# Projection operands 14 columns later, low weight parts 64 bytes later, one tile of ones in place of two

## The chip, the cores and the metric

The kernel runs on one core of one Trainium2 chip. The metric is the device time of one execution in microseconds (us); lower is better. Names used below: TensorE is PE (matmuls) with its weight loads as PEld; VectorE is DVE, ScalarE is ACT, GpSimd is POOL, SyncE is SP. L295 is line 295 of the kernel. SBUF is the memory on the chip, 128 partitions side by side; PSUM is where matmuls write their sums.

## What is computed

One layer of a hybrid decoder over 16 learned tokens and 1024 tokens of 1024 channels (T = 1040), in float32. Cut to what matters:

```python
h = layer_norm(concat([meta, x]), g, b)
z = h @ w_in + b_in                      # split into q | k | v | conv input | two gates
a = swa_sink_attention(q, k, v, ...)     # 8 heads of 64, window 128
y_attn = a @ w_attn_proj                 # 512 -> 1024
c = c_val * sigmoid(c_gate)
c = silu(layer_norm(causal_dwconv(c), g, b))
y_conv = c @ w_conv_proj                 # 512 -> 1024
mixed = sigmoid(g_attn) * y_attn + sigmoid(g_conv) * y_conv
h = layer_norm(ALPHA * h + mixed @ w_out, g, b)
up = causal_dwconv(h @ ffn_w_up); u, g = split(up)
out = layer_norm(ALPHA * h + (gelu(g) * u) @ ffn_w_down, g, b)
```

## The kernel before, in words

**Three products for one.** To keep float32 accuracy at the faster rate of the float32r format, an operand is split into a high part (the value rounded to float32r) and a low part (what is left). One product of two operands is then three matmuls: high weights by high operand (L295), high weights by low operand (L299), low weights by high operand (L300). The function `product` issues these three for each chunk k of 128 channels, and all of them add up in one PSUM tile. In a matmul one operand of 128 x 128 is loaded into PE first (the weights, a LDWEIGHTS in the profile), and the other one, 128 x up to 512 columns, streams past it (the moving operand). The load for the next matmul runs while the present one streams.

**The z stage** (from about 57 us to 416 us, L303 to L882). There are 30 tiles of 128 output channels of z. For each, `weights` (L274) takes a raw tile of 128 x 1024 from the pool `wraw`, loads it by SP, takes two tiles `whi` and `wlo` from the pool `wsp`, and splits: ACT copies the high part, DVE or, from the 24th tile, POOL subtracts for the low part. Only the third tile, which is used while a later one is already loading, has tiles of its own. `z_group` (L303) then makes 24 matmuls (8 chunks of three) for each of three groups of columns: ZG (0 to 400, 400 to 784, 784 to 1040), or TG, whose first group begins at column 14. The normalised input lies in the tiles RHO (chunks 0 to 3) and RHC (4 to 7) in slots of T = 1040 columns, high and low parts in turn. The attention over eight blocks of queries and the depthwise convolution (31 multiply-adds of 1026 columns per chunk on DVE, L663) run between these tiles. The sum over the conv chunks (L882) is split (L893, L894) and multiplied by a tile of ones on PE (L885, L886) for the mean; squares follow the same way (L946 to L949), then scaling, the activation, and the split into OC (L972, L973). Attention results are scaled and split into OA (L984 to L986).

**The projections** (416 to 514 us, L1071 to L1118). OA holds the attention result, OC the conv result: four chunks each, in eight slots of T columns, high and low in turn, of which columns 0 to 1026 of a slot are used. Eight tiles of weights (`weights` again, with both projections in one tile) are multiplied with four groups of columns, PG: 0 to 258, 258 to 514, 514 to 770, 770 to 1026. For each group 12 matmuls read OA and 12 read OC. `merge` multiplies with the gates on DVE.

**What follows.** Output rows (`out_rows`, 514 to 611 us), the up projection (L1481, to about 1052 us; seven products per block of channels in place of eight, each of 12 matmuls of 258 columns and 12 of 256), the down projection (L1614, 512 columns). They reuse OA, OC, RHO and RHC with offsets of their own, and the `wsp` tiles: `prep_wo` for two chunks of `w_out` (L1051), a ring of split weights in the up projection (L1299), rows of gains and sums in the down projection (L1637).

**What sets the order.** A scheduler places the instructions of each engine in a fixed order, by the ranks that the code sets (`rank`, `tc.cur_priority`); extra edges (`after`, `pin`, `line`) fix the order in places. Each engine then works through its own list and waits for the others by semaphores.

**Memory.** Pools on the left side, in this order: const, small, wraw, wsp, arena (FA, RHC, RHO, OB), and OA behind them. Each tile in `wsp` is 128 x 1024 (4096 bytes in a partition), two buffers for each of the two tags. Two tiles of ones, 128 x 128, lie in const: `ones` in float32, filled by DVE (L222) and used by 28 matmuls at the start (L535), and `ones_r` in float32r, copied from it by ACT (L892) and used for the means.

Of the kernel before, what the change touches and what calls it, by code (L numbers as in the profile page):

```python
# [23 lines left out]
F = mybir.dt.float32  # L24
R = mybir.dt.float32r
# [4 lines left out]
P = 128  # L30
D = 1024
KC = D // P
NMETA = 16
S = 1024
T = S + NMETA
U0 = 14
# [65 lines left out]
def tile_hybrid_layer(  # L102
# [3 lines left out]
    nc = tc.nc  # L106
# [5 lines left out]
    def load(o, i):  # L112
        return nc.sync.dma_start(out=o, in_=i)
# [5 lines left out]
    def f32(ap):  # L119
        return ap.bitcast(F)  # L120

    def after(ins, first):

        tc.add_manual_dep(ins.ins, first.ins.name, mybir.DependencyInfo(
            mybir.DependencyClass.NoSync, mybir.DependencyReason.SCHED_ONLY), reason="order of work")

    @contextmanager
    def rank(p):

        saved = tc.cur_priority  # L130
        tc.cur_priority = p
        yield
        tc.cur_priority = saved


    const = ctx.enter_context(tc.tile_pool(name="const", bufs=1, side="left"))
    small = ctx.enter_context(tc.tile_pool(name="small", bufs=4, side="left"))
    wraw_p = ctx.enter_context(tc.tile_pool(name="wraw", bufs=2, side="left"))
    wsp_p = ctx.enter_context(tc.tile_pool(name="wsp", bufs=2, side="left"))
# [28 lines left out]
    sp = start.enter_context(tc.tile_pool(name="start", bufs=1, side="right", reuse_waits="tile"))  # L168
# [49 lines left out]
    ffw = lambda t, c: cff[:, t * 44 + c:t * 44 + c + 1]  # L218

    ones_r = const.tile([P, P], R, name="ones_r")  # L220
    ones = const.tile([P, P], F, name="ones")
    nc.vector.memset(ones, 1.0 / CW)  # L222
    qb = const.tile([P, 4], F, name="qb")
    half_ = const.tile([P, 1], F, name="half")
# [34 lines left out]

    tc.cur_priority = RK_QKV  # L260

    def wraw(shape):
        return wraw_p.tile(shape, F, name="wr", tag="wr")

    def split(raw, hi, lo, quick=False, behind=None):
        ins = nc.scalar.copy(hi, raw)  # L266
        if behind is not None:
            after(ins, behind)
        return (nc.vector if quick else nc.gpsimd).tensor_tensor(lo, raw, f32(hi), OP.subtract)  # L269
# [4 lines left out]
    def weights(shape, fill):  # L274
        fills[0] += 1
        n = fills[0]
        own = n == 3
        raw = sp.tile(shape, F, name="wr3") if own else wraw(shape)
        with rank({1: 13, 2: 18, 3: 17, 4: 23}.get(n, RK_SPLIT)):
            last_fill.append(fill(raw))  # L280
        hi, lo = (sp.tile(shape, R, name=t + "3") if own else wsp_p.tile(shape, R, name=t, tag=t)
                  for t in ("whi", "wlo"))
        if n <= 3:
            return hi, lo, raw
        with rank(RK_SPLIT):
            last_split.append(split(raw, hi, lo, n <= 23))
        return hi, lo
# [22 lines left out]
    def z_tile(fill, groups, evac, wt=None):  # L310
        wt = wt or weights([P, KC, P], fill)
        for g, (a, b) in enumerate(groups):
            z_group(wt, g, a, b, evac)
# [156 lines left out]
    def parts(g, *ks, hi_act=()):  # L470
        a, b = HG[g]
        for k in ks:
# [5 lines left out]
            dv(V.tensor_tensor(h0(k, 1, a, b), tm, f32(h0(k, 0, a, b)), OP.subtract))  # L478

    first = [weights([P, KC, P], in_cols(m)) for m in (4, 5, 0)]  # L480
    evacs0 = [k_evac, v_evac, q_evac(0)]

# [125 lines left out]

    tc.cur_priority = RK_QKV + 3000
    wt_c1 = [weights([P, KC, P], in_cols(m)) for m in (11, 7)]  # L610
    tc.cur_priority = RK_RESID
    residual(3, -1, 0, 1, 2, 3)
# [93 lines left out]
    for q4 in range(2):  # L706
        ps = pat.tile([P, 512], F, name="ps_v4", tag="t", bufs=2)
        for i in range(4):
            c = NMETA + (q4 * 4 + i) * P
            nc.tensor.transpose(ps[:, i * P:(i + 1) * P], vT[:, c:c + P], ident)  # L710
        src = ps[:, :].rearrange("p (n g d) -> p n g d", g=2, d=HD)
        for g in range(NKV):
            hi, lo = (V[:, q4 * 4:q4 * 4 + 4, g, i] for i in range(2))
# [30 lines left out]
    for h in range(NH):  # L744
        g, r = divmod(h, 4)
        o = ps[:2, h * 16:(h + 1) * 16]
# [137 lines left out]
    def mean_mms(ps, w, hi, lo):  # L884
        nc.tensor.matmul(ps, w, hi, start=True, stop=False)  # L885
        nc.tensor.matmul(ps, w, lo, start=False, stop=True)  # L886
# [2 lines left out]
    c_hi = cp.tile([P, 16 + T], R, name="c_hi", tag="cin")  # L889
    c_lo = Kx[0].rearrange("p n c -> p (n c)")[:, :U]  # L890
    with rank(RK_EVAC):
        nc.scalar.copy(ones_r, ones)  # L892
        nc.scalar.copy(c_hi[:, :U], csum)  # L893
        pinned.append(nc.vector.tensor_tensor(c_lo, csum, f32(c_hi[:, :U]), OP.subtract))  # L894
        for g, (a, b) in enumerate(UG):
            means[g] = pat.tile([P, 512], F, name="ps_m", tag="st"[g % 2], bufs=2)
            mean_mms(means[g][:, :b - a], ones_r, c_hi[:, a:b], c_lo[:, a:b])
# [6 lines left out]
    OC = late.tile([P, 8320], R, name="OC")  # L904
# [8 lines left out]
    def temp(n):  # L913
        return tmp_p.tile([P, 386], F, name="t", tag="t", bufs=6)[:, :n]


    def conv(c, hl, a, b):
        o = (c * 2 + hl) * T
        return OC[:, o + a:o + b]

    def pin(ins):

        if pinned:
            after(ins, pinned[-1])
        pinned.append(ins)
# [9 lines left out]
    def cln_var(g):  # L935
        a, b = UG[g]
        n = b - a
        s_ = temp(n)
        nc.scalar.activation(s_, acc[0][:, a:b], AF.Square)
        for c in range(1, CH):  # L940
            q_ = temp(n)
            nc.scalar.activation(q_, acc[c][:, a:b], AF.Square)
            pin(dve.tensor_tensor(s_, s_, q_, OP.add))

        hi, lo = (OC[:, i * T + a:i * T + b] for i in (2, 3))
        pin(dve.tensor_copy(hi, s_))  # L946
        pin(dve.tensor_tensor(lo, s_, f32(hi), OP.subtract))
        sums[g] = pat.tile([P, 512], F, name="ps_m", tag="s", bufs=2)
        mean_mms(sums[g][:, :n], ones_r, hi, lo)  # L949
# [24 lines left out]


    def oo(r, hl, a, b):
        o = (r * 2 + hl) * T
        return OA[:, o + a:o + b]

    def o_split(g, r):  # L980
        a, b = UG[g]
        n, x = b - a, 2 if g == 0 else 0
        t = o_all[:, r, a:b]
        pin(dve.tensor_tensor(t[:, x:], t[:, x:], inverse[r][:, a + x - 2:b - 2], OP.mult))  # L984
        pin(dve.tensor_copy(oo(r, 0, a, b), t))
        pin(dve.tensor_tensor(oo(r, 1, a, b), t, f32(oo(r, 0, a, b)), OP.subtract))  # L986
# [7 lines left out]
    cln_centre(0)  # L994
    cln_centre(1)
    cln_var(0)
    cln_centre(2)
    cln_var(1)
    cln_rstd(0)
    cln_scale(0)  # L1000
    cln_var(2)
    cln_rstd(1)
    cln_scale(1)
# [41 lines left out]
    def prep_wo(k, raw=None, behind=None):  # L1045
        if k < 4:
            hi, lo = OA[:, k * 2048:k * 2048 + 1024], OA[:, k * 2048 + 1024:k * 2048 + 2048]
        elif k < 6:
            hi, lo = ((RX, RW)[k - 4][:, x:x + 1024] for x in (0, 1024))
        else:  # L1050
            hi, lo = (wsp_p.tile([P, D], R, name=n, tag=n) for n in ("whi", "wlo"))  # L1051
        if raw is None:
            raw = wraw([P, D])
            load(raw, w_out_v[k])
        split(raw, hi, lo, k < 4, behind)
        wo[k] = (hi, lo)
# [16 lines left out]
    for m in range(KC):  # L1073
        hi, lo = weights([P, KC, P], lambda raw: load(raw, w_ab[m]))
# [37 lines left out]
        if m in (2, 3):  # L1112
            raw = (FA[:, 4112:5136], OB[:, 3072:4096])[m - 2]
            load(raw, w_out_v[m + 2])
            prep_wo(m + 2, raw, last_act)
# [38 lines left out]
    def line(ins):  # L1154

        if lined:
            after(ins, lined[-1])
        lined.append(ins)
        return ins
# [129 lines left out]
    RING = [RHO[:, i * 1024:(i + 1) * 1024] for i in range(4)]  # L1289
# [4 lines left out]
    def wsplit(src):  # L1294
        i = ring_next[0]
        ring_next[0] += 1
        i %= len(RING)
        if RING[i] is None:
            RING[i] = wsp_p.tile([P, D], R, name="ws", tag=("whi", "wlo")[i % 2])  # L1299
        t = RING[i]  # L1300
        hi, lo = t[:, 0:512], t[:, 512:1024]
        nc.scalar.copy(hi, src)  # L1302
        ins = nc.vector.tensor_tensor(lo, src, f32(hi), OP.subtract)  # L1303
        if pinned_w[0]:
            line(ins)
        elif ring_next[0] <= 10:
            after(ins, formed[0])
        return hi, lo
# [7 lines left out]
    def up_weights():  # L1316


        def tt(*x):
            ins = nc.vector.tensor_tensor(*x)  # L1320
            if pinned_w[0]:
                line(ins)

        rows = w_rows(0)
        for c in range(FC):
            a11, a12, a21, a22 = rows
            yield wsplit(a11)
            yield wsplit(a12)
            p4 = wsplit(a22)
            tt(a22, a21, a22, OP.add)  # L1330
            tt(a21, a11, a21, OP.subtract)
            tt(a11, a22, a11, OP.subtract)
            yield wsplit(a11)
            yield p4
            yield wsplit(a22)
            tt(a22, a12, a11, OP.subtract)
            yield wsplit(a21)
            p3 = wsplit(a22)
            if c + 1 < FC:
                rows = w_rows(c + 1)  # L1340
            yield p3
# [117 lines left out]
    for c in range(FC):  # L1459
        V4, X, Z, Y = (pup.tile([P, 1024], F, name=n, tag=n) for n in ("pw", "px", "pz", "py"))  # L1460
        passes = ((1,), (0,)) if c == 0 else ((0, 1),)
        for subs in passes:
            last = subs == passes[-1]
            w_next = iter(range(7))
            a, b = SUB[subs[0]][0], SUB[subs[-1]][1]
# [168 lines left out]
    extra = []  # L1634

    def ln_rows(names):
        return [wsp_p.tile([P, D], F, name=n, tag=t) for n, t in zip(names, ("whi", "wlo"))]  # L1637

    gains = ln_rows(("g1", "b1"))
    g1, b1 = gains  # L1640
# [127 lines left out]
```

## Time and profile before

| | us |
|---|---|
| median of 3 runs | 1271.26 |
| lowest, highest | 1271.07, 1271.75 |
| profiled execution | 1270.77 |
| its span on the core | 1268.5 |

How to read it: the profile shows one execution. A row of the timeline has the start, the duration, the engine, the line, the operation, what is written from what, the shapes and a count. Matmuls overlap in the profile, because each is shown with its way through the array: the time that one costs is the distance to the start of the next. Groups show busy time, the mean duration of one in ns, and the idle time before them. Waits show who waited for whom, the sum in us, the number of times, and the longest. A row of windows shows PE, weight loads, DVE, ACT and POOL as busy us with their counts, then the clock granted to PE, the busy share of the DMA engines and GB/s. The chain is the path of work that ended last, with equal neighbours merged. Times in these rows count from the start of the span.

### The profile page before, as it was taken

Reading aid. Unit: us, or ns where it says so; the run is one execution under the profiler, and the core shown is the slowest. Engines: PE = TensorE matmul, PEld = TensorE weight load, DVE = VectorE, ACT = ScalarE, POOL = GpSimd, SP = SyncE. Lnnn points to the kernel's source line nnn. Section 1 sums busy time; section 2 is a strip of 40 time slices with the busy share of each in tenths; the row PEclk is TensorE's granted clock in tenths of the full one; section 3 lists DMA queues with packets and bytes.
Section 4 is the critical chain, followed back from the end, with each engine's and each line's share of the span. In section 5 each row is a group of like instructions: output and inputs, shape, how many; then the busy total and the mean of one; then the engine's idle time right before and its main releaser. Section 6 shows DMA issues by size and latency. Waiting matters only on the chain.

```text
span 1268.5 us, 21682 instructions
## 1 busy us (share of the span) xinstructions
PE 1257.3 (99%) x8546; PEld 1190.5 (94%) x8546; DVE 1084.0 (85%) x1837; ACT 588.3 (46%) x1066; POOL 53.1 (4%) x28
## 2 busy tenths in 40 slices
PE   9999999999999999999999999999999999999997
PEld 8999999999999999788899999999999998888886
DVE  7899989999989577548999999988889887896697
ACT  7522254645573233335665555554455544445330
POOL 0000000010122232000000000000000000000000
PEclk9999999999999999999999999999999999999999
DMA  7294633332156554222145546453454558989722
GB/s 276 74 308 104 187 94 98 103 96 85 68 147 174 166 160 124 84 83 83 67 148 195 199 173 211 164 208 121 163 204 170 191 202 292 382 324 342 245 87 83
DMA packets 96152, 212.10 MB, mean 167 GB/s; under 512 B 10787, under 2 KB 35939, under 8 KB 95922
## 3 DMA queue, kind: packets, MB, share of 16 engines
q1 hardware_dynamic: 84282, 199.64, 46.9%
q10 hardware_dynamic: 11768, 11.08, 2.7%
q8 instruction: 67, 1.10, 0.4%
q14 instruction: 35, 0.29, 0.1%
HBM read 150.29 MB, written 62.70 MB: 168 GB/s over the span
## 4 chain that ended last, share of the span: by engine, by line
PE 98%; DVE 1%; ACT 0%; DMA 0%; issue 0%; SPq 0%; DVEq 0%
PE px L1481 15%; PE py L1481 10%; PE ps_x L1614 9%; PE ps_z L299 8%; PE ps_z L295 8%; PE ps_z L300 8%; PE ps_z L1614 7%; PE pw L1481 5%; PE pz L1481 5%; PE ps_p L299 2%; PE ps_p L295 2%; PE ps_p L300 2%; PE ps_w L295 2%; PE ps_w L300 2%; PE ps_w L299 2%; PE ps_z L511 2%
## 5 line engine op out<-in xcount | busy, mean ns | idle before, releaser
L663 DVE SCALAR_TENSOR_TENSOR FA<-cin,cols,FA 128x1026 f32<-128x1026 f32 x120 | 155.2, 1305 | 0.2
L295 PE MATMUL ps_z<-RHO,whi 128*128 128x384 f32 (+2 forms) x324 | 104.7, 323 | 0.0
L299 PE MATMUL ps_z<-RHC,whi 128*128 128x384 f32 (+2 forms) x324 | 104.7, 323 | 0.0
L299 PE MATMUL ps_z<-RHO,whi 128*128 128x384 f32 (+2 forms) x324 | 104.0, 321 | 0.0
L295 PE MATMUL ps_z<-RHC,whi 128*128 128x384 f32 (+2 forms) x324 | 103.9, 321 | 0.0
L300 PE MATMUL ps_z<-RHC,wlo 128*128 128x384 f32 (+2 forms) x324 | 103.6, 320 | 0.0
L300 PE MATMUL ps_z<-RHO,wlo 128*128 128x384 f32 (+2 forms) x324 | 103.3, 319 | 0.0
L1303 DVE TENSOR_TENSOR RHO<-wr,RHO 128x512 fp32r<-128x512 f32 x94 | 63.7, 686 | 9.5 <-ACT RHO L1302 9.5
L1302 ACT CAST RHO<-wr 128x512 fp32r<-128x512 f32 x94 | 56.6, 619 | 20.9 <-DVE wr L1320 11.8
L266 ACT CAST whi<-wr 128x1024 fp32r<-128x1024 f32 x37 | 38.9, 1051 | 57.2 <-PE ps_z L299 36.5
L295 PEld LDWEIGHTS ps_z<-RHO,whi 128*128 128x128 f32 x324 | 60.9, 188 | 0.5 <-issue 0.3
L299 PEld LDWEIGHTS ps_z<-RHC,whi 128*128 128x128 f32 x324 | 60.9, 188 | 0.4
L300 PEld LDWEIGHTS ps_z<-RHC,wlo 128*128 128x128 f32 x324 | 61.0, 188 | 0.2
L300 PEld LDWEIGHTS ps_z<-RHO,wlo 128*128 128x128 f32 x324 | 60.9, 188 | 0.1
L295 PEld LDWEIGHTS ps_z<-RHC,whi 128*128 128x128 f32 x324 | 60.8, 188 | 0.2
L299 PEld LDWEIGHTS ps_z<-RHO,whi 128*128 128x128 f32 x324 | 60.9, 188 | 0.1
L1320 DVE TENSOR_TENSOR wr<-wr 128x512 f32<-128x512 f32 x88 | 60.4, 686 | 0.2
L1493 ACT COPY FA<-px 128x514 f32<-128x514 f32 (+2 forms) x23 | 13.1, 572 | 81.8 <-PE px L1481 81.8
L269 POOL TENSOR_TENSOR wlo<-wr,whi 128x1024 fp32r<-128x1024 f32 x17 | 41.3, 2429 | 188.3 <-ACT whi L266 178.6
L670 ACT ACTIVATE FA<-ps_z,cols 128x386 f32<-128x386 f32 (+2 forms) x48 | 26.0, 541 | 46.6 <-PE ps_z L300 45.8
L1303 DVE TENSOR_TENSOR ws<-wr,ws 128x512 fp32r<-128x512 f32 x60 | 40.7, 687 | 5.5 <-ACT ws L1302 5.4
L1481 PE MATMUL px<-OA,RHO 128*128 128x258 f32 x324 | 43.3, 282 | 0.0
(467 smaller groups left out, 3582.9 us busy)
## 6 DMA issues: line engine op xcount, KB each, us to landing
wr<-in_w_up_dram SPq DMA_DIRECT2D x44, 512.0 KB, 4.2
wr<-in_w_z_dram SPq DMA_DIRECT2D x30, 512.0 KB, 3.7
fd<-FA SPq DMA_DIRECT2D x44, 256.0 KB, 2.5
OB<-in_w_down_dram SPq DMA_DIRECT2D x19, 512.0 KB, 5.5
qt<-qd SPq DMA_DIRECT2D x28, 256.0 KB, 3.9
td<-OB SPq DMA_DIRECT2D x12, 512.0 KB, 3.2
sums<-fd SPq DMA_DIRECT2D x12, 512.0 KB
sd<-sums SPq DMA_DIRECT2D x12, 512.0 KB, 2.8
```

What stands on the lines that cost most here:

```text
L266: ins = nc.scalar.copy(hi, raw)
L269: return (nc.vector if quick else nc.gpsimd).tensor_tensor(lo, raw, f32(hi), OP.subtract)
L295: ins = nc.tensor.matmul(ps, ah, bh, start=i == 0, stop=False)
L299: nc.tensor.matmul(ps, ah, bl, start=False, stop=False)
L300: last = nc.tensor.matmul(ps, al, bh, start=False, stop=i == n - 1)
L663: nc.vector.scalar_tensor_tensor(acc[c], cin[:, j:j + U], wc, acc[c], OP.mult, OP.add)
L670: nc.scalar.activation(t, ps, AF.Tanh, bias=bcol(14 + i), scale=0.5)
L1302: nc.scalar.copy(hi, src)
L1303: ins = nc.vector.tensor_tensor(lo, src, f32(hi), OP.subtract)
L1320: ins = nc.vector.tensor_tensor(*x)
L1481: ins = nc.tensor.matmul(o, x[:, ks], bmat(sub, q, hl, k), start=first and k + j == 0, stop=k == 3 and j == 2, skip_group_check=not first)
L1614: nc.tensor.matmul(banks[i], l[:, ts], r[:, ws], start=first and a and x + k == 0, stop=z and x == len(ops) - 1 and k == 2, skip_group_che ...
```

## The change

Five edits, one diff:

- The slots of OA and OC keep their size, but what is written and read lies U0 = 14 columns (56 bytes) later in each: `conv`, `oo`, and the sums of squares, which borrow two slots of OC.
- Tiles with the tag `wlo` are 64 columns (256 bytes) longer. `weights` uses them from column 16 on (64 bytes later); all other users from column 0.
- New helpers `wsp` and `pair_of` make these tiles.
- `ones` is the same memory as `ones_r`, seen as float32; the copy on ACT is gone. Const is 512 bytes shorter, wsp 512 bytes longer.
- Nothing else moves: tiles between the two lie 512 bytes earlier, the second `wlo` buffer 256 bytes earlier, the arena and all behind it where they were.

```diff
     ones_r = const.tile([P, P], R, name="ones_r")
-    ones = const.tile([P, P], F, name="ones")
+    ones = f32(ones_r)
     nc.vector.memset(ones, 1.0 / CW)
...
+    def wsp(name, tag):
+        return wsp_p.tile([P, D + (64 if tag == "wlo" else 0)], R, name=name, tag=tag)
+
+    def pair_of(hi, lo, shift=0, shape=None):
+        hi, lo = wsp(hi, "whi"), wsp(lo, "wlo")[:, shift:shift + D]
+        return [t.rearrange("p (k c) -> p k c", k=KC) for t in (hi, lo)] if shape else [hi, lo]
...
-        hi, lo = (sp.tile(shape, R, name=t + "3") if own else wsp_p.tile(shape, R, name=t, tag=t)
-                  for t in ("whi", "wlo"))
+        hi, lo = (sp.tile(shape, R, name=t + "3") for t in ("whi", "wlo")) if own else pair_of("whi", "wlo", 16, shape)
...
-        nc.scalar.copy(ones_r, ones)
         nc.scalar.copy(c_hi[:, :U], csum)
...
     def conv(c, hl, a, b):
-        o = (c * 2 + hl) * T
+        o = (c * 2 + hl) * T + U0
         return OC[:, o + a:o + b]
...
-        hi, lo = (OC[:, i * T + a:i * T + b] for i in (2, 3))
+        hi, lo = (conv(1, hl, a, b) for hl in range(2))
...
     def oo(r, hl, a, b):
-        o = (r * 2 + hl) * T
+        o = (r * 2 + hl) * T + U0
         return OA[:, o + a:o + b]
...
-            hi, lo = (wsp_p.tile([P, D], R, name=n, tag=n) for n in ("whi", "wlo"))
+            hi, lo = pair_of("whi", "wlo")
...
-            RING[i] = wsp_p.tile([P, D], R, name="ws", tag=("whi", "wlo")[i % 2])
+            RING[i] = wsp("ws", ("whi", "wlo")[i % 2])[:, 0:D]
...
     def ln_rows(names):
-        return [wsp_p.tile([P, D], F, name=n, tag=t) for n, t in zip(names, ("whi", "wlo"))]
+        return [wsp_p.tile([P, D + (64 if t == "wlo" else 0)], F, name=n, tag=t)[:, 0:D]
+                for n, t in zip(names, ("whi", "wlo"))]
```

## The prediction

> **What bounds the kernel now.** I read the page first, for the engine that ends last, then the waits of that engine, then the busy time by stage.
>
> ```profile
> span 1268.5 us, 21682 instructions
> PE 1257.3 (99%) x8546; PEld 1190.5 (94%) x8546; DVE 1084.0 (85%) x1837; ACT 588.3 (46%) x1066; POOL 53.1 (4%) x28
> PEclk9999999999999999999999999999999999999999
> PE 98%; DVE 1%; ACT 0%; DMA 0%; issue 0%; SPq 0%; DVEq 0%
> ```
>
> The chain that ended last is 98% PE, at the full granted clock throughout. The waits of PE, all there are:
>
> ```profile
> PE ps_w L535 <- DVE ones L222: 1.1, 1, 1.1
> PE pw L1481 <- ACT FA L1283: 1.0, 1, 1.0
> PE ps_h L461 <- DVE xn L425: 0.8, 1, 0.8
> PE ps_z L508 <- ACT FA L467: 0.3, 1, 0.3
> ```
>
> They sum to 3.2 us. So a nanosecond per matmul is a nanosecond of the end, unless PE then arrives somewhere before its data. Busy time by stretch, from 90 us (z tiles and attention), from 350 (last gate tiles), from 416 (the two projections, then output rows):
>
> ```profile
> 90.00:348.00 258.00, 258.00 (x1703) 253.19 (x1702) 247.57 (x452) 117.55 (x291) 9.23 (x4) 1.00 0.39 106
> 350.00:416.00 66.00, 66.00 (x423) 65.78 (x422) 58.97 (x112) 36.86 (x57) 12.72 (x6) 1.00 0.59 172
> 416.00:514.00 98.00, 98.00 (x793) 97.14 (x792) 68.03 (x136) 27.50 (x54) 24.25 (x10) 1.00 0.47 132
> ```
>
> PE and its weight loads (second and third figure) fill all three. The fourth is DVE: 247.57 of 258 us before 348, a second limit close behind; 68 of 98 us in the projections, where it has room.
>
> **What a matmul costs here** is its distance to the next start, since they overlap. From the timeline, the second projection tile (first group, the other three groups = 72 matmuls, next tile):
>
> ```profile
> 428.03 0.28 PE L295 MATMUL ps_p<-OA,whi 128*128 128x258 f32 x1
> ...
> 430.93 0.29 PE L295 MATMUL ps_p<-OA,whi 128*128 128x256 f32 x1
> ...
> 439.65 0.28 PE L295 MATMUL ps_p<-OA,whi 128*128 128x258 f32 x1
> ```
>
> 24 matmuls of 258 columns in 2.90 us are 120.8 ns each; 72 of 256 in 8.72 us are 121.1. The last z tile, whose groups are 24 matmuls each:
>
> ```profile
> 405.14 0.34 PE L295 MATMUL ps_z<-RHO,whi 128*128 128x386 f32 x1
> ...
> 409.37 0.34 PE L295 MATMUL ps_z<-RHO,whi 128*128 128x384 f32 x1
> ...
> 413.58 0.28 PE L295 MATMUL ps_z<-RHO,whi 128*128 128x256 f32 x1
> ...
> 416.40 0.28 PE L295 MATMUL ps_p<-OA,whi 128*128 128x258 f32 x1
> ```
>
> That is 176.3, 175.4 and 117.5 ns. And the up projection (12 per row) and a run of the down projection:
>
> ```profile
> 741.77 1.58 PE L1481 MATMUL pw<-OA,ws 128*128 128x258 f32 x12
> 743.19 1.57 PE L1481 MATMUL pw<-RHC,ws 128*128 128x256 f32 x12
> 744.60 1.59 PE L1481 MATMUL py<-OA,ws 128*128 128x258 f32 x12
> ...
> 751.75 1.52 PE L1481 MATMUL py<-RHC,RHO 128*128 128x256 f32 x12
> 753.10 1.60 PE L1481 MATMUL px<-RHC,RHO 128*128 128x258 f32 x12
> ```
> ```profile
> 1099.82 10.20 PE ps_x L1614 x45
> ```
>
> The same 256 columns take (744.60 - 743.19)/12 = 117.5 in one block and (753.10 - 751.75)/12 = 112.5 in another, against 121.1 in the projections; 512 columns take 10.20/45 = 226.7, which halves to 113.3. Shape, engine and clock are the same; what differs is where operands lie. The row with 113.3 per 256 columns I call the floor (0.443 ns a column: 170.0 for 384). z lies about 5 ns above it, the projections 7.8.
>
> **Where the operands lie.** RHO, RHC, OA, OC and the weight tiles start 64 bytes past a multiple of 128. A slot of 1040 columns is 4160 = 65 x 64 bytes, so a low part lies 64 bytes off its high part, modulo 128. The projections' groups start at columns 0, 258, 514, 770; 258 x 4 = 1032 = 16 x 64 + 8. So today the three later groups are read from bytes 72 (high) and 8 (low) of a 128-byte line. 14 columns later they start at 272, 528, 784, all multiples of 16 columns: bytes 0 and 64. The first group goes from 64 and 0 to 120 and 56. Low weights go from byte 64 to byte 0.
>
> **The change, part by part.** (1) *Three aligned groups of the projections.* 8 tiles x 3 groups x 24 = 576 matmuls. After it they lie exactly as z's 256-column group lies today (0 and 64), which is the nearest row: 117.5. Saving 576 x (121.1 - 117.5) = 2.1 us. Ends: nothing, and the floor, 576 x 7.8 = 4.5 us.
>
> (2) *The first group*, 192 matmuls, now off the 64-byte grid. z's 386-column group begins at bytes 120 and 56 too, and stands at 176.3 against 175.4 for 384: two columns at 0.443 make the 0.9. So being off costs nothing there, and I take 0. Ends: 258 columns at (743.19 - 741.77)/12 = 118.3 would save 192 x 2.5 = 0.5 us; as much the other way.
>
> (3) *Low weights 64 bytes later*, for the z tiles and the projections. While one product streams, the weights of the next load. Per chunk: high weights with the high part, high with the low, low with the high. Today the moving operand flips by 64 bytes after the first and after the second product while the loads stay at 64; only from the third to the next first nothing flips. Once low weights lie 64 bytes off, each pair of stream and load lies the same way round, in all three. Does the unflipped product cost less? By mean durations (third column: L300 is the third product):
>
> ```profile
> L295 PE MATMUL ps_z<-RHO,whi 128*128 128x384 f32 x108 | 36.9, 342 | 0.0
> L299 PE MATMUL ps_z<-RHO,whi 128*128 128x384 f32 x108 | 36.7, 340 | 0.0
> L300 PE MATMUL ps_z<-RHO,wlo 128*128 128x384 f32 x108 | 36.3, 336 | 0.0
> L295 PE MATMUL ps_z<-RHO,whi 128*128 128x256 f32 x108 | 30.6, 283 | 0.0
> L299 PE MATMUL ps_z<-RHO,whi 128*128 128x256 f32 x108 | 30.4, 281 | 0.0
> L300 PE MATMUL ps_z<-RHO,wlo 128*128 128x256 f32 x108 | 30.2, 280 | 0.0
> L295 PE MATMUL ps_p<-OA,whi 128*128 128x256 f32 x96 | 27.4, 285 | 0.0
> L1481 PE MATMUL px<-OC,RHO 128*128 128x256 f32 x324 | 42.5, 279 | 0.0
> L1481 PE MATMUL py<-RHC,RHO 128*128 128x256 f32 x156 | 19.8, 276 | 0.0
> ```
>
> It does: 336 beside 342 and 340, 280 beside 283 and 281. Duration is not distance: the last three rows go with 121.1, 117.5 and 112.5, so a nanosecond of duration stands for 0.6 (285 to 279) to 1.0 (285 to 276) of distance; I take 0.6, the step that part 1 makes. If all three were as the third, 384 columns gain (6 + 4)/3 x 0.6 = 2.0 ns, 256 gain 0.8, and I give the first group the same 0.8: 1.2 on average. z has six rows of 324 matmuls, 1944 in all: 2.3 us. Ends: nothing, and the floor, about 5 x 1944 = 9.7 us.
>
> Not all of that reaches the end. In PE's fixed order stand the sums for the conv branch's mean, whose input is the conv on DVE:
>
> ```profile
> 345.64 1.05 ACT L893 CAST c_hi<-csum 128x1026 fp32r<-128x1026 f32 x1 [1.57 <-DVE csum L882]
> 346.72 1.23 DVE L894 TENSOR_TENSOR kx<-csum,c_hi 128x1026 fp32r<-128x1026 f32 x1 [1.12 <-ACT c_hi L893]
> 348.00 0.55 PEld L885 LDWEIGHTS ps_m<-c_hi,ones_r 128*128 128x128 f32 x3
> ...
> 349.71 0.37 PEld L886 LDWEIGHTS ps_m<-kx,ones_r 128*128 128x128 f32 x2
> ```
> ```profile
> L886 PE MATMUL ps_m<-OC,ones_r x3: 280/336/340, 360.8 to 371.9; 128*128 128x386 f32 x1, 128*128 128x384 f32 x1, 128*128 128x256 f32 x1
> ```
>
> c_hi is there at 346.69, PE comes at 348.00: 1.3 us of room. c_lo is there at 347.95, PE at 349.71: 1.8. DVE, 96% busy up to there, hardly comes earlier. So of the gain before 348 I count 1.3 us; what is more waits behind L885, with every later z matmul queued behind it. After the last sums (371.9) PE is free of that chain: 44.5 us of z at 11.26 us and 72 matmuls a tile are 284 matmuls, 0.3 us.
>
> (4) *One tile of ones.* The copy of the ones goes:
>
> ```profile
> L892 ACT CAST ones_r<-ones 128x128 fp32r<-128x128 f32 x1 | 0.3, 281 | 0.0
> ```
>
> 0.281 us of an engine at 46%, whose result is first read at 348.00: 0 either way. The fill that PE's first matmul waits for (1.1 us) stays as large. 512 bytes saved, 2 x 256 added: nothing from the arena on moves.
>
> (5) *Everything else* writes as many elements through the same instructions; no DMA is added or moved on any queue, no wait is added. I take 0. The splits on POOL and DVE are hidden by PE, which waits for none of them.
>
> The sum: 2.1 + 0 + 1.3 + 0.3 = 3.7 us. The profiled execution took 1270.77 us (span 1268.5 and 2.3 around it), 0.49 below the median 1271.26; from the median I get 1267.6.
>
> [...]
>
> **The rivals.** *Nothing happens* (the change doesn't do what it says): the distance depends on something other than these bytes, such as what ran before. For: the two blocks of 256 columns in the up projection lie alike, modulo 128, and still differ by 5 ns. 1271.3. *Moving operand only:* part 1 works, low weights don't matter: 1269.2. For: only 0.8 ns in z's 256 columns. *The floor:* streams and loads fall into step as in the down projection, where nothing flips: 4.5 us in part 1, 284 x 5 = 1.4 after 371.9, 1.3 before: 7.2 us, 1264.1; a little lower if DVE, too, comes earlier. Against: at one fixed relation most up-projection blocks stay at 117.5. *Slower:* the fixed relation is the bad one in z's first group, whose high part and high weights then both lie in the same half of the line always, instead of every other time. Price: at the projections' present 7.8 ns above the floor, 2.8 more than now, 648 x 2.8 = 1.8 us is not enough; it decides from 648 x 3.7 = 2.4 us, and if z's other groups follow (1944 x 2.8 = 5.4, less 2.1) the time is 1274.6. For: the projections show that distances above z's exist. Against: 512 columns with stream and load both at byte 64 run at the floor.
>
> **How the numbers follow.** Forecast 0.38 (gains of 2.6 to 5.5 us), floor 0.20, moving operand only 0.16, nothing 0.12, slower 0.14. 0.2%, about what a measurement of this kernel can tell from no change, is 2.5 us: faster 0.38 + 0.20 = 0.58, same 0.16 + 0.12 = 0.28, slower 0.14. The range 1262.0 to 1272.5 holds the forecast, "only", "nothing" and most of the floor, and leaves out the slower rival and the lowest end of the floor.
>
> **What would show it.** Part 1: the 72 matmuls of a projection tile take 8.46 us instead of 8.72. Part 2: its first 24 stay at 2.90. Part 3: L295, L299 and L300 at 384 columns come together near 336 to 338, a last z tile of 11.2 us or less, and a wait of PE at L885 for c_hi if z gained over 1.3 us. A longer z tile, or an unchanged 8.72, would make the prediction wrong; so would a new wait of PE behind 514 us that takes the gain back.

## The result, and the profile after

| kernel | median, us | ratio to before, 95% interval | span of the profiled execution, us |
|---|---|---|---|
| before, same chip | 1271.15 | | 1268.5 |
| after | 1269.18 | 0.9984 [0.9978, 0.999] | 1267.2 |

Medians are of 22 runs each; one run of after, at a granted clock of 0.75, took 1542.23 us and is left out of the ratio. The change gains 1.97 us, 0.16%. The interval leaves no doubt about the sign, and the size lies inside the 0.2% that the prediction called "about what a measurement of this kernel can tell from no change". First the page of after and the waits of PE (total, times, longest, in us):

```profile
span 1267.2 us, 21681 instructions
PE 1255.8 (99%) x8546; PEld 1188.9 (94%) x8546; DVE 1084.1 (86%) x1837; ACT 588.5 (46%) x1065; POOL 54.0 (4%) x28
```
```profile
PE ps_w L541 <- DVE ones_r L222: 1.1, 1, 1.1
PE pw L1486 <- ACT FA L1288: 1.0, 1, 1.0
PE ps_h L467 <- DVE xn L431: 0.6, 1, 0.6
PE ps_z L514 <- ACT FA L473: 0.3, 1, 0.3
PE px L1486 <- ACT OB L1498: 0.2, 1, 0.2
PE ps_z L301 <- ACT FA L676: 0.2, 1, 0.2
```

PE still fills 99%. Two waits of 0.2 us are new. ACT has 1065 instructions in place of 1066: the copy of the ones. (Lines of after: L301, L305, L306 are L295, L299, L300 of before; L676 is L670.) The same three stretches as before, in windows (PE is the second figure):

```profile
90.00:348.00 258.00, 258.00 (x1705) 253.26 (x1704) 247.53 (x451) 117.11 (x291) 9.34 (x4) 1.00 0.38 107
350.00:416.00 66.00, 65.78 (x419) 65.37 (x418) 59.09 (x112) 36.86 (x57) 13.96 (x6) 1.00 0.61 169
416.00:514.00 98.00, 98.00 (x806) 96.98 (x805) 69.45 (x139) 28.77 (x56) 24.36 (x11) 1.00 0.48 135
```

From 90 to 348 us PE does 1705 matmuls where it did 1703: nothing gained to speak of. Between 350 and 416 PE now lacks 0.22 us. In the projections it does 806 in place of 793: this is where the time came from. The second projection tile and the last z tile, in the timeline:

```profile
428.44 0.28 PE L301 MATMUL ps_p<-OA,whi 128*128 128x258 f32 x1
...
431.32 0.28 PE L301 MATMUL ps_p<-OA,whi 128*128 128x256 f32 x1
...
439.80 0.28 PE L301 MATMUL ps_p<-OA,whi 128*128 128x258 f32 x1
```
```profile
405.77 0.34 PE L301 MATMUL ps_z<-RHO,whi 128*128 128x386 f32 x1
...
410.04 0.34 PE L301 MATMUL ps_z<-RHO,whi 128*128 128x384 f32 x1
...
414.25 0.28 PE L301 MATMUL ps_z<-RHO,whi 128*128 128x256 f32 x1
...
417.08 0.28 PE L301 MATMUL ps_p<-OA,whi 128*128 128x258 f32 x1
```

The first group of the projection takes 2.88 us (2.90 before), the other 72 matmuls 8.48 (8.72 before), 117.8 ns each. The z tile takes 11.31 us (11.26 before): 4.27, 4.21 and 2.83 in place of 4.23, 4.21 and 2.82. The groups by shape (busy us, mean ns of one):

```profile
L301 PE MATMUL ps_z<-RHO,whi 128*128 128x384 f32 x108 | 36.8, 341 | 0.0
L305 PE MATMUL ps_z<-RHO,whi 128*128 128x384 f32 x108 | 36.7, 340 | 0.0
L306 PE MATMUL ps_z<-RHO,wlo 128*128 128x384 f32 x108 | 36.2, 335 | 0.0
L306 PE MATMUL ps_p<-OA,wlo 128*128 128x256 f32 x96 | 27.0, 281 | 0.0
L305 PE MATMUL ps_p<-OA,whi 128*128 128x256 f32 x96 | 26.9, 281 | 0.0
L301 PE MATMUL ps_p<-OA,whi 128*128 128x256 f32 x96 | 26.8, 279 | 0.0
```

In z the three products keep their order, 341, 340 and 335; they did not come together. In the projections L301 falls from 285 to 279. (These are mean durations, not distances.)

For all that follows I use the length of two stages in each kernel's trace, from start to start: z, from the first matmul of L300/L306 to the first of `ps_p`, and the projections, from there to the matmul that follows the last one. The start of z lies between 56.8 and 57.4 us, and these lengths leave that variation out. Where a stage's operands lay at the same places, its length came out within 0.1 us from kernel to kernel, so they tell apart what medians don't.

| stage, us | before | after | difference |
|---|---|---|---|
| z | 359.34 | 359.64 | +0.30 |
| projections | 97.76 | 95.59 | -2.17 |
| up and down projection, first to last start | 648.96 | 649.19 | +0.23 |

The last row is the wait at L1498, which stands in no other kernel's trace (648.9 to 649.0 in all of them), so it belongs to this execution. The first two give -1.87 of the 1.97 us. Within the projections, the eight first groups of 24 matmuls give 0.21 of the 2.17 us (mean distance 119.6 ns in place of 120.7), the three later groups 1.96 (117.8 in place of 121.2).

### The profile page after: what moved, and what is told of

Read it like the earlier page. It is cut to its first block, busy times and chain, and to the rows that moved or that the text cites. A ratio compares the mean times of both kernels' runs of the same rounds, so it can differ in the third digit from the quotient of the medians.

```text
span 1267.2 us, 21681 instructions
## 1 busy us (share of the span) xinstructions
PE 1255.8 (99%) x8546; PEld 1188.9 (94%) x8546; DVE 1084.1 (86%) x1837; ACT 588.5 (46%) x1065; POOL 54.0 (4%) x28
## 4 chain that ended last, share of the span: by engine, by line
PE 96%; ACT 1%; DVE 1%; DMA 1%; issue 0%; SPq 0%; ACTq 0%; DVEq 0%
PE px L1486 15%; PE py L1486 10%; PE ps_x L1619 9%; PE ps_z L305 8%; PE ps_z L301 8%; PE ps_z L306 8%; PE ps_z L1619 7%; PE pz L1486 5%; PE pw L1486 5%; PE ps_p L306 2%; PE ps_p L301 2%; PE ps_p L305 2%; PE ps_w L306 2%; PE ps_w L301 2%; PE ps_w L305 2%; PE ps_z L517 2%
## 5 line engine op out<-in xcount | busy, mean ns | idle before, releaser
L301 PE MATMUL ps_z<-RHO,whi 128*128 128x384 f32 (+2 forms) x324 | 104.7, 323 | 0.2 <-ACT FA L676 0.2
L305 PE MATMUL ps_z<-RHC,whi 128*128 128x384 f32 (+2 forms) x324 | 104.5, 323 | 0.0
L305 PE MATMUL ps_z<-RHO,whi 128*128 128x384 f32 (+2 forms) x324 | 104.0, 321 | 0.0
L306 PE MATMUL ps_z<-RHC,wlo 128*128 128x384 f32 (+2 forms) x324 | 103.8, 320 | 0.0
L301 PE MATMUL ps_z<-RHC,whi 128*128 128x384 f32 (+2 forms) x324 | 103.7, 320 | 0.0
L306 PE MATMUL ps_z<-RHO,wlo 128*128 128x384 f32 (+2 forms) x324 | 103.4, 319 | 0.0
L301 PEld LDWEIGHTS ps_z<-RHO,whi 128*128 128x128 f32 x324 | 60.9, 188 | 0.9 <-ACT FA L676 0.4
L305 PEld LDWEIGHTS ps_z<-RHC,whi 128*128 128x128 f32 x324 | 60.9, 188 | 0.4
L306 PEld LDWEIGHTS ps_z<-RHC,wlo 128*128 128x128 f32 x324 | 60.9, 188 | 0.2
L301 PEld LDWEIGHTS ps_z<-RHC,whi 128*128 128x128 f32 x324 | 60.9, 188 | 0.2
L306 PEld LDWEIGHTS ps_z<-RHO,wlo 128*128 128x128 f32 x324 | 61.0, 188 | 0.1
L305 PEld LDWEIGHTS ps_z<-RHO,whi 128*128 128x128 f32 x324 | 60.9, 188 | 0.1
L1498 ACT COPY FA<-px 128x514 f32<-128x514 f32 (+2 forms) x23 | 13.1, 572 | 80.7 <-PE px L1486 80.7
L676 ACT ACTIVATE FA<-ps_z,cols 128x386 f32<-128x386 f32 (+2 forms) x48 | 26.0, 542 | 46.6 <-PE ps_z L306 45.4
```

The source lines that it names most:

```text
L301: ins = nc.tensor.matmul(ps, ah, bh, start=i == 0, stop=False)
L305: nc.tensor.matmul(ps, ah, bl, start=False, stop=False)
L306: last = nc.tensor.matmul(ps, al, bh, start=False, stop=i == n - 1)
L676: nc.scalar.activation(t, ps, AF.Tanh, bias=bcol(14 + i), scale=0.5)
```

## The experiments

Two theories at the start. **The prediction's:** the three groups gain because their starts come to lie on multiples of 64 bytes, and low weights gain because each pair of stream and load then lies the same way round. **The rival** "moving operand only": the streams do it all, the weights nothing; its 1269.2 is what was measured. Edits are against after, unless it says otherwise. Times in brackets are ratios to before in the same round, where it took 1270.73 to 1270.82 us.

**1 and 2. Each half by itself.** `e1_slots_only` takes the shift of the low weights back (`"wlo", 0, shape` in `weights`):

> The changed kernel, with low weights back at the start of their tiles (64 bytes earlier): the 14 columns stay, the longer tiles and the one tile of ones too. Theory A (only where the moving operand starts counts): as the changed kernel, 2.0 us under the kernel before; the projections' 72 matmuls of 256 columns still take 8.48 us a tile. Theory B (stream and load must lie the same way round, so that 14 columns and 64 bytes only work together): at most half of it, under 1 us, and the 72 matmuls at 8.6 us or more. Theory A also says that the z stage, which the shift does not help, stays within 0.5 us of the kernel before.

`e2_low_only` takes the 14 columns back (`o = (c * 2 + hl) * T` in `conv`, the same in `oo`):

> The changed kernel, with the slots' 14 columns taken back: low weights stay 64 bytes later. Theory A: nothing, within 0.5 us of the kernel before, the projections' 72 matmuls near 8.72 us. Theory B: not decided by the sum, but the three products of the projections change their distances by more than 1 ns each. The forecast on record would have had 1.6 us from the z stage here; the profile after says about 0.

Measured: 1269.78 (0.9993 [0.9984, 1.0001]) and 1270.64 (0.9999 [0.9991, 1.0008]). The second projection tile of the first and of the second kernel:

```profile
428.24 0.29 PE L301 MATMUL ps_p<-OA,whi 128*128 128x258 f32 x1
...
431.15 0.28 PE L301 MATMUL ps_p<-OA,whi 128*128 128x256 f32 x1
...
439.71 0.29 PE L301 MATMUL ps_p<-OA,whi 128*128 128x258 f32 x1
```
```profile
428.39 0.28 PE L301 MATMUL ps_p<-OA,whi 128*128 128x258 f32 x1
...
431.32 0.28 PE L301 MATMUL ps_p<-OA,whi 128*128 128x256 f32 x1
...
439.96 0.28 PE L301 MATMUL ps_p<-OA,whi 128*128 128x258 f32 x1
```

The 72 matmuls take 8.56 us with the slots alone and 8.64 with the weights alone, against 8.72 in before and 8.48 with both. By stage: 96.51 us (-1.24) and 97.38 (-0.38); both together -2.17, which is 0.55 more than the two apart. So the rival falls too: it has the right time, but more than 0.9 of the 2.17 us hang on where the low weights lie. The total with the slots alone, 0.95 us under before, doesn't decide by itself (its interval holds 1); the stage does.

Which product gains is seen in the distances, from the starts in the timeline (the three later groups, seven tiles): 117.5, 120.0 and 119.2 ns for L301, L305 and L306 with the slots alone, 116.9, 117.7 and 118.8 with both. Most of the gain stands in L305; in after, the loads of the low weights start a median of 3 ns behind its matmuls. The loads' own records are as long in both (median 188 ns). The z stage took 359.67 without the shift and 359.64 with it: for z as a whole the weights' place is worth nothing.

**3 to 5. Which grid?** The slots 6, 10 and 12 columns later in place of 14. The later groups then start 32, 48 and 56 bytes past a multiple of 64. The line in `conv` for six, the same in `oo`:

```diff
-        o = (c * 2 + hl) * T + U0
+        o = (c * 2 + hl) * T + 6
...
```

> The changed kernel with 6 columns in place of 14: the three later groups start 32 bytes past a multiple of 64. Theory A with a grid of 64 bytes: the gain is lost, within 0.7 us of the kernel before, 72 matmuls near 8.7 us. Rival, a grid of 32 or 16 bytes: the gain stays, 2.0 us under the kernel before and 8.48 us.

> The changed kernel with 10 columns in place of 14: the three later groups start 48 bytes past a multiple of 64, a multiple of 16 but not of 32. Theory A with a grid of 64 bytes: within 0.7 us of the kernel before, 72 matmuls near 8.7 us. [...] Kernel e3 and this one both gaining says 16; e3 alone says 32; neither says 64.

> The changed kernel with 12 columns in place of 14: the three later groups start 56 bytes past a multiple of 64, that is 8 bytes past a multiple of 16, as in the kernel before, but elsewhere in the line. Theory C (kernels with 6, 10 and 14 columns all gained: what counts is the grid of 16 bytes, since 256 columns that start on it fill 64 lines of 16 bytes and off it touch 65, two of them in part): the gain of the slots is lost, the projections' stage near 97.4 us as in the kernel with low weights alone (before 97.8, changed 95.6), in all within 0.7 us of the kernel before. Rival D (any move of the slots against the weights gains): 95.4 to 96 us, about 1.8 us under the kernel before.

Measured: 1269.16 (0.9987 [0.9978, 0.9996]), 1268.72 (0.9985 [0.9976, 0.9994]) and 1270.2 (0.9995 [0.9987, 1.0004]); projections 95.88, 95.43 and 96.99 us. Six and ten columns gain about as much as fourteen, without a multiple of 64 bytes; twelve loses 1.4 us of it. The tile with twelve:

```profile
428.17 0.28 PE L301 MATMUL ps_p<-OA,whi 128*128 128x258 f32 x1
...
431.06 0.28 PE L301 MATMUL ps_p<-OA,whi 128*128 128x256 f32 x1
...
439.71 0.28 PE L301 MATMUL ps_p<-OA,whi 128*128 128x258 f32 x1
```

8.65 us for the 72. What separates twelve from the others is a grid of **16 bytes**: it starts 8 bytes off it. 256 columns are 1024 bytes, 64 steps of the grid when they start on it, and off it they touch 65. The 258 columns of the first group are 1032 bytes and touch 65 either way, and its 2.88 or 2.89 us in these three kernels fit that count. That the count is the reason is an estimate of the author's from these times; the price that the runs show is 2.1 to 2.8 ns a matmul (mean distances with the low weights shifted: 119.9 and 120.1 off the grid, in experiment 2 and with twelve columns; 117.8 with six and fourteen and 117.3 with ten).

**6. High weights shifted as well**, so that both lie at byte 0 (`ln_rows` gets tiles of the same length):

```diff
-        return wsp_p.tile([P, D + (64 if tag == "wlo" else 0)], R, name=name, tag=tag)
+        return wsp_p.tile([P, D + 32], R, name=name, tag=tag)
...
-        hi, lo = wsp(hi, "whi"), wsp(lo, "wlo")[:, shift:shift + D]
+        hi, lo = (wsp(n, t)[:, shift:shift + D] for n, t in ((hi, "whi"), (lo, "wlo")))
...
```

> The changed kernel with the high weights 64 bytes later, too (both tags 128 bytes longer): loads now lie at byte 0 of the line for high and low, as before they lay at 64 for both; the 14 columns stay. If the low weights' 0.9 us in the projections (96.5 us without them, 95.6 with) come from stream and load lying the same way round in all three products, it goes: 96.5 us, about 1.0 us under the kernel before, and z's groups of 386 columns are back at 176.2 ns from 178.0. If it comes from the place of the low weights alone, it stays: 95.6 us, 2.0 us under.

Measured: 1270.22 (0.9996 [0.9988, 1.0005]), projections 96.03, between after (95.59) and the slots alone (96.51); z 360.06, and the output rows behind the projections 97.67 in place of 96.98. It settles nothing: equal places of the two weights lose a part in the projections, not all; z's groups of 386 columns went back to 175.8 ns from 178.0, as "the same way round" would have it, but z as a whole became longer, and the longer high tiles moved other things as well.

**7. The grid in z.** The gate tiles' groups moved off the grid of 16 bytes by two columns (`[(14, 402), (402, 786), (786, 1040)]` in place of TG):

> The changed kernel with the gate tiles' inner group bounds at 402 and 786 in place of 400 and 784 (388, 384 and 254 columns instead of 386, 384 and 256): in 16 of the 30 z tiles the second and third group now start 8 bytes past a multiple of 16. Theory C: 16 x 48 = 768 matmuls pay as those of the projections did, about 3.3 ns each: 2.5 us slower than the changed kernel, so 0.3 to 0.7 us slower than the kernel before; z's 384 columns in gate tiles at 178 to 179 ns in place of 175. [...]

Measured: 1270.15 (0.9996 [0.9987, 1.0005]), z 361.07, 1.43 us more than after. The direction holds, the size is smaller than expected: 384 columns off the grid cost 176.7 ns in place of 173 to 176, and 254 columns 117.0, which is what two columns less than 256 (117.8) make by themselves. Those 254 start off the grid and end on it: 64 steps, as for 256.

**8. Ten columns, low weights shifted in the projections alone** (`"wlo", 16 if n > 30 else 0, shape`):

> 10 columns in place of 14, and low weights 64 bytes later in the projections' eight tiles alone, not in z's: by the runs so far the projections' stage takes 95.4 us (before 97.8) and z's 386 columns are back at 176.2 ns from 178.0. z's clean groups then cost what they did before; the sum is 2.3 to 2.6 us under the kernel before, a little better than either the changed kernel or the one with 10 columns. If z loses 0.3 us all the same, that loss is not the low weights' but a wait.

Measured: 1268.7 (0.9985 [0.9976, 0.9994]), projections 95.44, z 359.67. z is as long without any shift of its weights, and it took 359.62 in experiment 2, without the slots: its +0.3 us comes from neither.

**9 and 10. Where z's 0.3 us come from.** What is left is the tile of ones. `e10_ones_only` is before with `ones = f32(ones_r)` and without the copy, and nothing else. `e9_ten_and_one_more_copy` is the kernel of 8 with an extra copy on ACT:

```diff
+        nc.scalar.copy(half_, half_)
         nc.scalar.copy(c_hi[:, :U], csum)
```

> This is the kernel with ten columns and low weights shifted in the projections alone (1268.7 us), with one extra copy on ACT of a single column onto itself, where the copy of the ones used to stand, so that ACT has as many instructions as before. Its z stage took 359.67 us, the one of before 359.34, with the same mean distances of the matmuls; the 0.3 us is a wait of PE for an evacuation by ACT at about 380 us. Theory 'ACT's program, one instruction shorter, comes late there': z takes 359.3 to 359.4 us, the wait is gone, the projections stay at 95.4, and the total is 1268.4. Rival 'the wait comes from elsewhere, from the fill of the tile of ones or from the longer tiles': z stays at 359.6 to 359.7, total 1268.7.

> The kernel before with one tile of ones in place of two, and nothing else of the change. Prediction on record: 0 either way. Theory of the wait behind ACT's missing instruction: z takes 359.6 to 359.7 us in place of 359.34, with a wait of 0.2 to 0.3 us of PE for an evacuation by ACT at about 380 us, and the projections stay at 97.76; the total is 0.3 us above before, less than the times can show. Rival 'the longer tiles cause the wait': z 359.34, no such wait.

Measured: 1268.73 (0.9984 [0.9975, 0.9992]), z 359.65; and 1271.07 (1.0001 [0.9992, 1.001]), projections 97.76, z 359.62. One tile of ones alone makes the whole 0.29 us. ACT's timeline of before, then of the kernel with the ones alone, with the matmul that follows:

```profile
374.51 0.33 ACTq L117 DMA_DIRECT2D sgd<-FA  x1
374.96 1.05 ACT L266 CAST whi<-wr 128x1024 fp32r<-128x1024 f32 x1 [0.47 <-ACT FA L670]
...
381.89 0.56 ACT L670 ACTIVATE FA<-ps_z,cols 128x386 f32<-128x386 f32 x1
```
```profile
382.57 0.39 PE L295 MATMUL ps_z<-RHO,whi 128*128 128x386 f32 x1
```
```profile
374.57 0.33 ACTq L117 DMA_DIRECT2D sgd<-FA  x1
375.30 1.06 ACT L266 CAST whi<-wr 128x1024 fp32r<-128x1024 f32 x1 [0.76 <-ACT FA L670]
...
382.24 0.56 ACT L670 ACTIVATE FA<-ps_z,cols 128x386 f32<-128x386 f32 x1
```
```profile
382.86 0.44 PE L295 MATMUL ps_z<-RHO,whi 128*128 128x386 f32 x1
```

From the end of the DMA issue to the cast ACT takes 0.12 us in before (374.84 to 374.96) and 0.40 in the other. From there on every row of ACT is late by about 0.3 us. The evacuation of 386 columns ends at 382.80 in place of 382.45, and PE's next matmul into that buffer starts behind it, at 382.86 in place of 382.57. Of this 0.29, 0.06 is a later start of z in this execution (57.124 against 57.067), and 0.23 is new; the remaining 0.05 of the stage's 0.29 is the distance to the next matmul, 0.28 in place of 0.23. After has the same picture, and there the wait is named:

```profile
375.61 1.05 ACT L273 CAST whi<-wr 128x1024 fp32r<-128x1024 f32 x1 [0.78 <-ACT FA L676]
...
382.55 0.56 ACT L676 ACTIVATE FA<-ps_z,cols 128x386 f32<-128x386 f32 x1
```
```profile
383.17 0.44 PE L301 MATMUL ps_z<-RHO,whi 128*128 128x386 f32 x1 [0.22 <-ACT FA L676]
```

Why ACT is late: count ACT's records in the trace from 0, semaphore instructions and DMA issues among them. In the kernel with the ones alone a semaphore instruction follows on record 574, the DMA issue, only after 0.33 us, and none of the semaphores that it waits for is updated in this time; two more instructions follow on records 958 and 1214 after 0.32, where the same neighbours in before are 0.04 apart. Before has such places behind records 1086 and 1342, where this kernel has 0.04. Behind 958 and 1214 the gaps stand in all thirteen changed kernels, with 0.32 us, and behind 574 in twelve of them, with 0.33 or 0.34; in experiment 7 ACT's order differs there, and record 574 is another instruction. Other gaps of this size move with their instruction: one of 0.33 us stands behind record 114 in before and behind 113 in the kernel with the ones alone. In before, record 574 is an evacuation of 0.56 us, and the DMA issue follows 0.03 us behind it; the semaphore instruction behind that issue comes after 0.04. The extra copy of experiment 9 didn't take the gap away, but it was no test: it took the place of a semaphore instruction, and ACT's list stayed at 1522 records, one less than in before. What sets these gaps is not shown; that they belong to places in ACT's list was the author's estimate from five of them, and no experiment bears it out.

**11. Two columns** in place of ten (16 bytes past a multiple of 64), with the weights as in 8:

> The kernel with ten columns and low weights shifted in the projections alone, with 2 columns in place of 10: the later three groups then start at 260, 516 and 772, 16 bytes past a multiple of 64 and on a grid of 16 bytes. Theory of the 16-byte grid: the projections take 95.4 to 95.9 us, total 1268.7 to 1269.2. Rival 'a grid of 32 bytes or more': about 97 us as with 12 columns, total 1270.2.

Measured: 1268.55 (0.9981 [0.9972, 0.999]), projections 95.25. The grid of 16 bytes holds.

**12. Low weights 32 bytes off in place of 64** (shift 8), with the slots as in 8:

> The kernel with ten columns and low weights shifted in the projections alone, with the shift 8 columns (32 bytes) in place of 16 (64 bytes). Theory of the prediction, that low weights have to lie half a 128-byte line off as the low parts do: the gain of the shift is lost in part, the projections take 96 to 96.5 us, total 1269.3 to 1269.8. Rival 'any place that is not the same as that of the high weights': 95.4 us, total 1268.7.

Measured: 1268.39 (0.9981 [0.9973, 0.999]), projections 95.14. Its tile:

```profile
427.89 0.28 PE L301 MATMUL ps_p<-OA,whi 128*128 128x258 f32 x1
...
430.76 0.28 PE L301 MATMUL ps_p<-OA,whi 128*128 128x256 f32 x1
...
439.18 0.28 PE L301 MATMUL ps_p<-OA,whi 128*128 128x258 f32 x1
```

8.42 us for the 72, 116.9 ns each, the least of all. The half of a 128-byte line on which part 3 argued (no run shows a line of that length) is thus not what counts in the projections: an offset that makes no pair "the same way round" gains more. The last two kernels have the lowest ratios, 0.9981 against 0.9984 for after. The intervals overlap; the 0.3 to 0.45 us in the projections are shown by the traces alone.

## Why the prediction was right or wrong

**The bound:** right. PE ran at 99% in before and after, in the other twelve kernels its waits sum to 2.4 to 3.3 us, and what its matmuls gained in the projections arrived at the end.

**Part 1 (-2.1 us):** the size was right, -1.96 us for the three later groups, and 8.48 us a tile where 8.46 was forecast. The reason was half right. The row taken as nearest, z's 256 columns at 117.5, named the level that was reached. But the slots by themselves bring the stage 1.24; the rest needs the low weights moved as well. And the grid on which a start has to lie is 16 bytes, not 64 (experiments 3, 4, 5 and 11).

**Part 2 (0):** right within its ends: the first groups gain 0.2 us in all (2.88 us a tile against 2.90). With the slots alone they stay as they were, 120.9 ns against 120.7, which fits the count of steps of 16 bytes: 258 columns touch 65 of them from either place. The 0.2 us come with the low weights.

**Part 3 (-1.6 us in z):** this step failed. It read the lower duration of the third product (336 beside 342 and 340) as the gain of a product that isn't flipped and let the other two follow. They stayed: 341, 340 and 335. z got nothing from the shift, 359.64 us with it and 359.67 without. The durations it read don't stand for distances here. At 256 columns RHO's three rows have 283, 281 and 280 ns, RHC's 280, 287 and 283; in the uninterrupted groups of before the distances, over both, are 117.1, 117.9 and 117.8 ns: the third is not the cheapest. In uninterrupted groups of 24, the mean distances moved both ways: 384 columns from 175.5 to 174.7 ns, 386 columns from 176.2 to 178.0. At 384 the second product gave most of it (178.4 to 176.8); at 386 the third, which had been the cheapest, went from 174.0 to 178.5, so that what the prediction wanted to extend was lost there. This is the direction of the "slower" rival, which put its price in this very group. Why the third product's duration is lower stays open. Where part 3 expected nothing of its own, in the projections, the shift is worth 0.9 us. The room of 1.3 us at the mean's sums was never used up, so that cap stays untested.

**Part 4 (0 either way):** wrong by 0.3 us, in the step "0.281 us of an engine at 46%". The work that went was hidden, as said; but with ACT's list one instruction shorter its cast at about 375 us came 0.40 us behind the DMA issue in place of 0.12, and PE's matmul behind the evacuation came 0.23 us later.

**Part 5 (0):** right, the up and down projections stay at 648.9 to 649.0 us, but for the one wait in the profiled execution of after.

**The sum.** -3.7 was forecast, -1.97 measured: -2.17 in the projections and +0.30 in z are -1.87. The gap of 1.73 is part 3's 1.6, part 4's 0.3 and 0.14 that part 1 lacked, less 0.21 in part 2 and 0.1 that the stages don't show. The outcome with the largest chance, more than 0.2% faster (0.58), didn't come. The range held the time only since it reached to the cases in which one part brings nothing: that is luck, not mechanism. The time by itself would have put the rival "moving operand only" in the right, 1269.2 against 1269.18; experiment 1 shows that it isn't.

**The place of the weights.** In experiment 1 and in after the moving operands lie at the same places, only the low weights don't, and the projections take 96.51 and 95.59 us. By that, the place of the loaded weights does bear on the distance of the matmuls here. How isn't shown.

## What to carry to other kernels

Where PE runs without gaps, compare the distance of matmuls of one shape between stages: a stage that lies above another can have time in it (here 121.1 against 117.5 ns for 256 columns, and 2.17 us of the projections), and moving its operands by a few columns, on a grid of 16 bytes and with the moved weights at another offset than the rest, is cheap to try. Take the level from a stage that has it, and take it in distances: a difference between durations need not be one of cost (here 283, 281 and 280 ns in RHO and 280, 287 and 283 in RHC went with 117.1, 117.9 and 117.8). With one tile of ones, and so one instruction less on ACT's list, z took 0.29 us longer here, so look for new waits even where the work was hidden.

## What the runs showed of the hardware

- In the projections a matmul of 256 float32r columns whose stream starts off a grid of 16 bytes took 2.1 to 2.8 ns more (119.9 and 120.1 against 117.3 and 117.8); in z, 254 columns that start off the grid and end on it took 117.0, against 117.8 for 256 on it.
- The time of the projections changed with the bytes where streams and weights lie (97.76 us in before, 96.51 with the slots moved, 95.59 with the low weights moved too), and it repeated: they took 95.43 and 95.44 us in two kernels with the same places (4, 8), 97.76 and 97.76 in two others (before, 10). Low weights 32 bytes off in place of 64 changed the stage by 0.3 us (95.14 and 95.44).
- Behind records 574, 958 and 1214 of ACT's list the next instruction came 0.32 to 0.34 us later in the changed kernels (behind 574 in twelve of thirteen), where the same neighbours in before are 0.04 apart; behind 1086 and 1342 it is the other way round. What sets these gaps isn't shown.
